# Preparing weight splits 2048 columns at a time, with the low part of 54 loads formed by an accumulating DMA

## The chip, the cores and the metric

The kernel runs on one core of one Trainium2 chip. The metric is the device time of one execution in microseconds (us), median over the runs. Lower is better.

## The reference, cut to what matters

Two transformer-like blocks act on 256 tokens of 1024 features in float32. The first has a chunked attention, a gated linear recurrence and a gated feed-forward layer, the second a gated token mixer, a stick-breaking attention and four gated feed-forward layers. Nearly all the arithmetic is products of activations with large weight matrices:

```python
u = jnp.einsum('bsd,de->bse', rmsnorm(h, g), w_in)      # 1024 x 7168
gate, up = jnp.split(h @ w_ffn_in, 2, axis=-1)          # 1024 x 5632, five times
x = x + scale * ((jax.nn.silu(gate) * up) @ w_ffn_out)  # 2816 x 1024, five times
```

The weights are used once each, so 250 MB of them stream through the core in one execution.

## The kernel before, in words

**Precision by splitting.** A weight w is split into a high part h, which is w rounded to the short float format fp32r, and a low part l = w - h. Activations are split in the same way. Each product is then three matmuls: h with the high activations, h with the low activations, and l with the high activations (`mm3`, L212 to L215). The third one of a triple is the first to need l.

**Groups.** `PLAN` (L67 to L93) lists 239 groups in the order of their use; a 240th load-sized transfer is there for the recurrence's gates. A group is one 1 MB load of 128x2048 weights (`raw`), made of two halves of 1024 columns. Most halves take 24 matmuls of 256 columns. Groups are numbered from 0; 40 to 72 are the first feed-forward layer, 73 to 105 the second, and so on. In a feed-forward layer two groups that write fresh `wk` banks (input weights) alternate with one group that adds to `acc` banks (output weights), so the pattern repeats every three groups.

**The weight pipeline.** SyncE (SP) issues the loads (`load`, L139), with three `raw` buffers. `prep` (L149 to L168) prepares one half: ScalarE copies `raw` to h (L162), and VectorE computes l = raw - h (L163). After the second half of a group its `raw` buffer is given up, and `load` issues the load three groups on. There are eight h buffers and eight l buffers of 1024 columns each. `refill` (L177) is called after each half that TensorE takes: it prepares up to two halves, as long as fewer than seven halves (four, for the first twelve halves) lie ahead of TensorE. So the second half of group g is asked for after the first half of group g-3, and the first half of group g half a group earlier.

**The order of the work.** The schedule is written by hand (`manual_schedule`): each engine runs its instructions in the order in which Python issues them. `group` (L199) issues a half's matmuls, then steps the generators that evict and process results (`rounds`, L184; two steps a half), then calls `refill`. So an engine's queue holds evictions and preparations in one fixed order, and an instruction that waits holds up all that stand behind it. In a feed-forward layer an eviction goes VectorE (L306, times the row factor), ScalarE (L738, silu), VectorE (L743), ScalarE (L309, high part), VectorE (L310, low part). GpSimd (POOL) does little: the power for the norms (`rpow`, L280), the loads of the attention bias (L467) and two fills behind each (L469), and three other small loads (L977, L982, L937).

**The start.** `block1` (L386 to L390) splits the inputs and prepares groups 0 and 1 in between, the first half in two pieces. Groups 2 and 3 are the first that `refill` prepares. The second feed-forward layer (L878) passes `more`, which keeps `refill` from preparing anything in some places (L750, L765), so that the statistics of two norms come first.

Of the kernel before, what the change touches and what calls it, by code (L numbers as in the profile page):

```python
# [9 lines left out]
F32 = mybir.dt.float32  # L10
F32R = mybir.dt.float32r
BF16 = mybir.dt.bfloat16
AF = mybir.ActivationFunctionType
# [7 lines left out]
NJ = FF // 128  # L21
NEG = -1e30

NB = 8
LA = NB - 1
NRAW = 3


# [38 lines left out]
def make_plan():  # L67
# [24 lines left out]

PLAN = make_plan()  # L93

PARAMS = [
    ("norm_mix_g", 8), ("conv_w", 32), ("conv_b", 8), ("b_r", 8), ("b_i", 8), ("lam", 8),
    ("b_merge", 16), ("norm_ffn_g", 8), ("final_norm_g", 8), ("ffn_norm", 32), ("mix_norm", 16),
# [9 lines left out]
class Builder:  # L107
# [14 lines left out]
        return self.ci // 2  # L122

    def take(self):
        h, l = self.hl.pop(self.ci)
        spec = PLAN[self.ci // 2][self.ci % 2]
        self.ci += 1
        return h, l, spec

    def sb(self, name, shape, dt=F32):  # L130
        return self.cp.tile(shape, dt, tag=name, name=name)
# [14 lines left out]
        if g == 4:  # L146
            self.nc.sync.dma_start(self.gw, self.dram["gates"])

    def prep(self, pieces=1):  # L149
        n = self.preps  # L150
        g, c = divmod(n, 2)
        if g >= len(PLAN):
            return
        self.preps += 1
        nc = self.nc
        raw = self.raw[g][:, c * 1024:(c + 1) * 1024]
        h = self.hlp.tile([128, 1024], F32R, tag="h", name="h")
        l = self.hlp.tile([128, 1024], F32R, tag="l", name="l")
        w = 1024 // pieces
        for i in range(pieces):  # L160
            s = slice(i * w, (i + 1) * w)
            nc.scalar.activation(h[:, s], raw[:, s], AF.Copy)  # L162
            nc.vector.tensor_tensor(l[:, s], raw[:, s], h[:, s].bitcast(F32), op=ALU.subtract)  # L163
        self.hl[n] = (h, l)
        if c == 1:
            del self.raw[g]
            if self.loads < g + 1 + NRAW:
                self.load()  # L168

    def spawn(self, gen):  # L170
        self.gens.append(gen)
# [2 lines left out]
        next(gen)  # L174
        self.gens.append(gen)

    def refill(self, most=2):  # L177
        """prepares the weights to come, more of them once the first loads have landed"""
        ahead = LA if self.ci > 12 else 4
        for _ in range(most):  # L180
            if self.preps < self.ci + ahead:
                self.prep()

    def rounds(self, n=2):  # L184
        for _ in range(n):
# [94 lines left out]
        self.nc.gpsimd.tensor_tensor(dst, src, self.mhalf[:, 0:src.shape[1]], op=ALU.pow)  # L280

    def bcast_mm(self, bank, half, col, start):
        """a factor per token (partition) to a row on every partition"""
        for t in range(2):
            self.mm(bank[:, half, t * 128:(t + 1) * 128], col[:, t:t + 1].to_broadcast([128, 128]), self.ident,
                    start and t == 0, True)

    def stats_a(self, pool=None, kv=False):
        """squares to the per-token factor column"""
        nc = self.nc  # L290
        self.st = (pool or self.acc)()
        self.R, self.rcol = (self.Rkv, self.rckv) if kv else (self.Rt, self.rc)
        self.stat_mm(self.sq[0], self.st, 0, True)
        nc.vector.tensor_scalar(self.v2, self.st[:, 0, 0:2], 1.0 / D, 1e-6, op0=ALU.mult, op1=ALU.add)
        self.rpow(self.rcol, self.v2)

    def stats_b(self):
        """the factors on every partition"""
        self.bcast_mm(self.st, 1, self.rcol, False)
        self.nc.scalar.activation(self.R, self.st[:, 1, :], AF.Copy)  # L300

# [58 lines left out]
        nc.gpsimd.memset(self.tiny, 2.0 ** -115)  # L360

    def warm_up(self):
        """keeps the tensor engine busy while the first operands are on their way"""
        nc = self.nc
        nc.vector.memset(self.SL["c"][:, 0:64], 0.0)
        junk = self.SL["c"][:, 0:64].bitcast(BF16)
        bank = self.wk()
        for _ in range(40):
            self.mm(bank[:, 0, 0:128], junk, junk, True, True)
        nc.scalar.preload_act_table_set("exp_and_others")  # L370
# [7 lines left out]
        for gi in range(2):  # L378
            self.group(kinds, lambda c, h, l, s: self.pe_k(h, l, s[2], self.XS, outs), fills=fills[gi])

    # ---------------------------------------------------------------- block 1
    def block1(self):
        nc, dram = self.nc, self.dram
        SA, SL, RR = self.SA, self.SL, self.RR
# [1 line left out]
        for p in range(4):  # L386
            self.split_h(p, self.X, g, self.XS)
            self.split_l(p, self.X, g, self.XS)
            self.prep(2 if p == 0 else 1)
        self.squares(self.X, self.sq)  # L390

        xr = SA.rearrange("p (a b) -> p a b", b=259)
# [6 lines left out]
        gb = SL["g"].rearrange("p (a b) -> p a b", b=256)  # L399
        ga = SL["h"].rearrange("p (a b) -> p a b", b=256)  # L400

        # xr
        w = ("A", "w_in")
        b = [self.wk(), self.wk()]
        self.start_k((("K", "w_in"),) * 2, [b[0][:, 0, :], b[0][:, 1, :], b[1][:, 0, :], b[1][:, 1, :]])
# [31 lines left out]
        for p in range(4):  # L437
            a_group(mul_ev(ga, p))

        # v, tokens on partitions  # L440
        V = SL["c"].rearrange("p (t c) -> p t c", c=1024)
        for cg in range(2):
            banks = [self.wk(), self.wk()]
# [9 lines left out]
                           lambda c, h, l, s: self.pe_nat(h, l, s[2], self.XS, banks),  # L453
                           end=(lambda: self.spawn(v_ev())) if gi else None)

        # attention state
        qk = self.carve("b", 0, 2, 512)
        PT = self.carve("b", 1024, 2, 384) + self.carve("d", 1536, 1, 384) + self.carve("f", 1536, 1, 384)
        bias = self.carve("d", 0, 2, 768)
# [82 lines left out]

        qk_group(0)

        # rnn_out
        accs = [self.acc() for _ in range(4)]
        for r in range(4):
            self.group((("R", "rnn_out"),) * 2,
# [10 lines left out]
        for j in range(1, 8):  # L559
            qk_group(j)  # L560

        # attn_out, merged with the recurrent branch
        accs2 = [self.acc() for _ in range(4)]
        MH, ML = RR[0], RR[1]
        for r in range(3):
# [13 lines left out]
        self.tail_group("attn_out", (6, 7), lambda k: (OH[:, k, :], OL[:, k, :]), accs2, merge, merge_l)  # L579
        self.drain()  # L580

        # w_o and the residual
        gf = lambda k: ("norm_ffn_g", k)
        for half in range(2):
            b = [self.wk(), self.wk()]
# [120 lines left out]
                    yield  # L706

    def tail_group(self, name, ks, zf, accs, fin, fin_l):
        """last two rows of weights, output by output, each pair finished as it comes"""
        g = self.gi  # L710
        assert [c[:3] for c in PLAN[g]] == [("R", name, k) for k in ks], (PLAN[g], name, ks)
        hl = [self.take()[:2] for c in range(2)]
        self.rounds(1)
        for p in range(4):
            for o in (2 * p, 2 * p + 1):
                for i, k in enumerate(ks):
                    s = slice(o * 128, o * 128 + 128)
                    zh, zl = zf(k)
                    self.mm3(accs[p][:, o % 2, :], hl[i][0][:, s], hl[i][1][:, s], zh, zl, start=False, stop=(i == 1))
            fin(p)  # L720
            if p:
                fin_l(p - 1)
        fin_l(3)
        self.rounds(1)
        self.refill()

    # ---------------------------------------------------------------- feed-forward
    def ffn(self, n, fin, fin_l, stats=None, nat=False, more=None):
        nc = self.nc
        a, r = ("A", f"{n}_in"), ("R", f"{n}_out")  # L730
# [56 lines left out]
        return accs  # L787

    def pe_rn(self, h, l, zh, zl, accs, first, last, banks=range(4)):
        """a row block of weights as the moving operand: tokens on partitions"""  # L790
        for b in banks:
            t, cg = divmod(b, 2)
            out = accs[b].rearrange("p a b -> p (a b)")
            s, ts = slice(cg * 512, cg * 512 + 512), slice(t * 128, t * 128 + 128)
            self.mm(out, zh[:, ts], h[:, s], first, False)
            self.mm(out, zh[:, ts], l[:, s], False, False)
            self.mm(out, zl[:, ts], h[:, s], False, last)
# [19 lines left out]
            self.split_l(p, self.X, g, xs)  # L817
        return fin, fin_l

    # ---------------------------------------------------------------- block 2  # L820
    def block2(self):
        nc, dram, P = self.nc, self.dram, self.par
        SA, SL, RR = self.SA, self.SL, self.RR

        # end of block 1: x2 = h * r1 * g1, next input x2 * r2 * g2
        XG = self.view("c", 4)

        def fin(p, bank):
# [71 lines left out]
        self.ffn("f3", fin, fin_l, stats=(lambda: self.stats_a(kv=True), sb3))  # L900
        self.squares(self.X, self.sq)

        # keys and values from the state before that feed-forward layer
        Kt = SL["c"][:, 0:512].rearrange("p (a b) -> p a b", b=256)
        Vt = SL["c"][:, 512:1024].rearrange("p (t c) -> p t c", c=256)
        kb, vb = self.acc(), self.acc()
# [33 lines left out]
        assert not self.gens  # L940

    def final_bank(self, b, bank):
        """the last norm and the output"""
        nc = self.nc
        t, cg = divmod(b, 2)
        flat = bank.rearrange("p a b -> p (a b)")
        part = lambda name, t, c: self.SL[name][:, (2 * t + c) * 512:(2 * t + c + 1) * 512]
        s0, s1, v, r = self.ss[:, t, 0:1], self.ss[:, t, 1:2], self.v2[:, t:t + 1], self.rc[:, t:t + 1]
        nc.scalar.activation(part("d", t, cg), flat, AF.Square, accum_out=s1 if cg else s0)  # L949
        nc.vector.tensor_tensor(part("f", t, cg), flat, self.gfin[:, cg * 512:(cg + 1) * 512], op=ALU.mult)  # L950
        if cg == 0:
            nc.vector.tensor_scalar(s0, s0, 1.0 / D, 1e-6, op0=ALU.mult, op1=ALU.add)
        else:
            nc.vector.tensor_scalar(v, s1, 1.0 / D, s0, op0=ALU.mult, op1=ALU.add)
            self.rpow(r, v)
        if b >= 2:
            t = b - 2
            r = self.rc[:, t:t + 1]
            nc.scalar.activation(part("f", t, 0), part("f", t, 0), AF.Copy, scale=r)  # L959
            nc.vector.tensor_scalar(part("f", t, 1), part("f", t, 1), r, None, op0=ALU.mult)  # L960
            for c in (1, 0):
                nc.sync.dma_start(self.dram["out"][t * 128:(t + 1) * 128, c * 512:(c + 1) * 512], part("f", t, c))

    def sgu(self, fin, fin_l):
# [29 lines left out]
                if c % 2:  # L994
                    yield

        # gate half, tokens on partitions
        def v_ev(banks, cg):
            sl = slice(cg * 512, (cg + 1) * 512)
            for t in range(2):  # L1000
# [42 lines left out]
        UH, UL = (RR[0], RR[1]), (RR[2], RR[3])  # L1043

        def mix(p):
            """token mixing of feature tiles 2p, 2p+1 and the product with u"""
            bank = self.wk()
            for f in range(2):
                c = 2 * p + f
# [203 lines left out]


def stick_order():
    """heads in the order of the tiles: two heads of neighbouring key/value heads each"""
    cols = []
    for T in range(8):
        kp, t = divmod(T, 4)
        for h in (2 * kp * 4 + t, (2 * kp + 1) * 4 + t):  # L1260
            cols.extend(range(h * 64, h * 64 + 64))
    return np.array(cols)
# [82 lines left out]
```

## Time and profile before

| what | us |
|---|---|
| median of the runs shown | 1462.57 |
| the runs (2) | 1462.52 and 1462.61 |
| profiled execution, span from first to last instruction | 1460.8 |
| TensorE busy in that span | 1451.3 |
| VectorE busy | 950.9 |
| ScalarE busy | 734.7 |
| GpSimd busy | 24.8 |

The profiled execution has no time of its own beside its span in what is shown; the median of the runs lies 1.8 us above the span, which is taken as what lies around it. Mean granted TensorE clock over the span: 0.999.

In the rows below, PE is TensorE's matmuls, PEld its weight loads, DVE VectorE, ACT ScalarE, POOL GpSimd and SP SyncE. "L163" is line 163 of the kernel. "l<-raw,h" means that l is written from raw and h. A timeline row begins with the start in us from the span's start and the length in us, and "x3" says that three like instructions in a row were merged into it.

### The profile page before, as it was taken

To read this page: it belongs to the slowest core of one execution; us is meant where nothing else is said; L and a number is where in the kernel's file an instruction comes from. 1 tells how busy PE (TensorE), PEld (TensorE's weight loads), DVE (VectorE), ACT (ScalarE), POOL (GpSimd) and SP (SyncE) were. 2 spreads that over 40 slices of the span, in tenths; PEclk is the share of its full clock that TensorE was granted. 3 is DMA by queue.
4 is the path that set the end of the run, shared out by engine and by line. 5 is a ranking of instruction groups with operands and counts; after the bars stand their busy time and mean duration, and the time that the engine had idled before them with its cause. 6 is when DMAs were issued, how large, how long until landed. Compare 5 with 4: busy or idle time off the path is not lost.

```text
span 1460.8 us, 26958 instructions
## 1 busy us (share of the span) xinstructions
PE 1451.3 (99%) x11548; PEld 1413.2 (97%) x11548; DVE 950.9 (65%) x1316; ACT 734.7 (50%) x1094; POOL 24.8 (2%) x57
## 2 busy tenths in 40 slices
PE   9999999999999999999999999999999999999998
PEld 9998999999999999998999999999999998999997
DVE  6976677665557765576775655567655576655563
ACT  5677465544445544455445444445444467544442
POOL 0000000000000000000000000000000000000000
PEclk9999999999999999999999999999999999999999
DMA  8555444454454555546444555544555542445451
GB/s 293 199 186 198 177 163 174 173 202 174 176 188 155 194 185 189 195 178 221 170 155 164 189 186 177 191 181 164 190 196 195 179 174 87 159 145 196 180 182 49
DMA packets 37624, 260.31 MB, mean 178 GB/s; under 512 B 4224, under 2 KB 4608, under 8 KB 7040
## 3 DMA queue, kind: packets, MB, share of 16 engines
q1 hardware_dynamic: 36288, 253.77, 48.7%
q0 software_dynamic: 1072, 4.72, 1.0%
q8 instruction: 90, 1.47, 0.4%
q14 instruction: 30, 0.25, 0.0%
q10 hardware_dynamic: 144, 0.10, 0.0%
HBM read 257.53 MB, written 1.05 MB: 177 GB/s over the span
## 4 chain that ended last, share of the span: by engine, by line
PE 99%; DMA 0%; ACT 0%; DVE 0%; SPq 0%; issue 0%; POOLq 0%; POOL 0%
PE wk L210 62%; PE acc L210 36%; DMA raw<-w 0%; PE acc L521 0%; PE wk L521 0%; ACT sf L959 0%; ACT sd L949 0%; DVE l L163 0%; ACT h L162 0%; SPq L352 0%; SPq L343 0%; DVE sf L950 0%; POOLq L1341 0%; POOL rc L280 0%; ACT sh L1134 0%
## 5 line engine op out<-in xcount | busy, mean ns | idle before, releaser
L163 DVE TENSOR_TENSOR l<-raw,h 128x1024 fp32r<-128x1024 f32 (+1 forms) x479 | 570.8, 1219 | 241.0 <-ACT h L162 240.4
L210 PE MATMUL wk<-xh,h 128*128 128x256 f32 x2272 | 646.8, 285 | 1.2 <-ACT h L162 1.2
L210 PE MATMUL wk<-xh,l 128*128 128x256 f32 x2272 | 643.9, 283 | 0.1
L210 PE MATMUL wk<-xl,h 128*128 128x256 f32 x2272 | 643.6, 283 | 0.0
L162 ACT ACTIVATE h<-raw 128x1024 fp32r<-128x1024 f32 (+1 forms) x479 | 485.7, 1044 | 64.6 <-PE acc L210 30.1
L210 PEld LDWEIGHTS wk<-xh,h 128*128 128x128 f32 x2272 | 436.7, 192 | 4.0 <-ACT h L162 1.8
L210 PEld LDWEIGHTS wk<-xl,h 128*128 128x128 f32 x2272 | 436.7, 192 | 0.5
L210 PEld LDWEIGHTS wk<-xh,l 128*128 128x128 f32 x2272 | 436.5, 192 | 0.6 <-DVE l L163 0.6
L210 PE MATMUL acc<-rr,h 128*128 128x256 f32 x2016 | 367.2, 284 | 0.0
L210 PEld LDWEIGHTS acc<-rr,h 128*128 128x128 f32 x2016 | 314.3, 192 | 1.9 <-issue 1.9
L210 PE MATMUL acc<-rr,l 128*128 128x256 f32 x1008 | 285.2, 283 | 0.0
L210 PEld LDWEIGHTS acc<-rr,l 128*128 128x128 f32 x1008 | 193.4, 192 | 0.0
L738 ACT ACTIVATE sa<-sa 128x256 f32<-128x256 f32 x110 | 45.4, 417 | 285.6 <-DVE sa L306 285.4
L309 ACT ACTIVATE rr<-sa 128x256 fp32r<-128x256 f32 (+1 forms) x122 | 52.7, 439 | 185.8 <-DVE sa L743 128.9
L306 DVE TENSOR_TENSOR sa<-wk,rt 128x512 f32<-128x512 f32 x92 | 62.3, 686 | 91.0 <-PE wk L210 73.1
L310 DVE TENSOR_TENSOR rr<-sa,rr 128x256 fp32r<-128x256 f32 (+1 forms) x122 | 54.2, 451 | 53.3 <-ACT rr L309 53.3
L210 PE MATMUL acc<-h,rr 128*128 128x512 f32 (+1 forms) x208 | 63.1, 374 | 0.0
L210 PEld LDWEIGHTS acc<-h,rr 128*128 128x128 f32 x208 | 38.7, 189 | 6.7
L258 ACT ACTIVATE xh<-x,par 128x256 fp32r<-128x256 f32 x56 | 25.2, 501 | 33.8 <-DVE x L316 18.6
L210 PE MATMUL acc<-l,rr 128*128 128x512 f32 (+1 forms) x104 | 38.9, 374 | 0.0
L743 DVE TENSOR_TENSOR sa<-sa 128x256 f32<-128x256 f32 x88 | 37.0, 428 | 0.0
L210 PE MATMUL wk<-rr,h 128*128 128x256 f32 x192 | 34.8, 283 | 0.0
(253 smaller groups left out, 970.2 us busy)
## 6 DMA issues: line engine op xcount, KB each, us to landing
raw<-w SPq DMA_DIRECT2D x237, 1024.0 KB, 4.9
sd<-bias POOLq DMA_DIRECT2D x8, 384.0 KB, 3.3
raw<-w SPq DMA_DIRECT2D x3, 512.0 KB, 8.3
sh<-gates SPq DMA_DIRECT2D x1, 1024.0 KB, 9.1
out<-sf SPq DMA_DIRECT2D x4, 256.0 KB, 2.1
x<-x SPq DMA_DIRECT2D x3, 256.0 KB, 7.4
raw<-w SPq DMA_DIRECT2D x2, 256.0 KB, 4.4
sa<-ws POOLq DMA_DIRECT2D x1, 512.0 KB, 3.7
```

The lines of the kernel that those rows point to most:

```text
L162: nc.scalar.activation(h[:, s], raw[:, s], AF.Copy)
L163: nc.vector.tensor_tensor(l[:, s], raw[:, s], h[:, s].bitcast(F32), op=ALU.subtract)
L210: self.nc.tensor.matmul(out, lhsT, rhs, start=start, stop=stop, skip_group_check=True)
L258: self.nc.scalar.activation(xs[0][:, k, :], src[p][:, f, :], AF.Copy, scale=self.par(*g(k)))
L306: self.nc.vector.tensor_tensor(dst, bank, self.Rpair(), op=ALU.mult)
L309: self.nc.scalar.activation(zh, src, AF.Copy)
L310: self.nc.vector.tensor_tensor(zl, src, zh.bitcast(F32), op=ALU.subtract)
L738: nc.scalar.activation(t[:, 0, :], t[:, 0, :], AF.Silu)
L743: nc.vector.tensor_tensor(t[:, 1, :], t[:, 0, :], t[:, 1, :], op=ALU.mult)
```

## The change

Each h and l buffer now holds a whole group: four buffers of 2048 columns in place of eight of 1024. `prep` prepares one group per call, `refill` calls it at most once per half, and the whole of group g is asked for after the first half of group g-3 (g-2 for the first twelve halves). The start keeps its pieces. For 54 groups, every fourth from 16 to 228, ScalarE first writes -h into the l buffer, then a DMA issued by GpSimd adds the raw weights to it (from the `raw` buffer for the 26 groups below 120, from HBM again for the 28 from 120 on), and ScalarE writes h. The other preparations are one ScalarE and one VectorE instruction of 2048 columns. Comments were removed.

```diff
-NB = 8
-LA = NB - 1
+NB = 4
 NRAW = 3
...
+DMA_L = {g: g < 120 for g in range(16, 232, 4)}
...
     def take(self):
-        h, l = self.hl.pop(self.ci)
-        spec = PLAN[self.ci // 2][self.ci % 2]
+        g, c = divmod(self.ci, 2)
+        h, l = (t[:, c * 1024:(c + 1) * 1024] for t in (self.hl.pop(g) if c else self.hl[g]))
         self.ci += 1
-        return h, l, spec
+        return h, l, PLAN[g][c]
...
-    def prep(self, pieces=1):
-        n = self.preps
-        g, c = divmod(n, 2)
-        if g >= len(PLAN):
+    def split(self, raw, h, l, s):
+        self.nc.scalar.activation(h[:, s], raw[:, s], AF.Copy)
+        self.nc.vector.tensor_tensor(l[:, s], raw[:, s], h[:, s].bitcast(F32), op=ALU.subtract)
+
+    def begin(self):
+        g = self.preps
+        self.preps += 1
+        self.hl[g] = tuple(self.hlp.tile([128, 2048], F32R, tag=n, name=n) for n in "hl")
+        return g
+
+    def release(self, g):
+        del self.raw[g]
+        if self.loads < g + 1 + NRAW:
+            self.load()
+
+    def prep(self):
+
+        if self.preps >= len(PLAN):
             return
...
+        g = self.begin()
+        raw, (h, l) = self.raw[g], self.hl[g]
+        if g in DMA_L:
+            self.nc.scalar.activation(l, raw, AF.Copy, scale=-1.0)
+            self.nc.gpsimd.dma_start(l, raw if DMA_L[g] else self.dram["w"][g], accum_op=ALU.add)
+            self.nc.scalar.activation(h, raw, AF.Copy)
+        else:
+            self.split(raw, h, l, slice(0, 2048))
+        self.release(g)
...
-    def refill(self, most=2):
-        """prepares the weights to come, more of them once the first loads have landed"""
-        ahead = LA if self.ci > 12 else 4
-        for _ in range(most):
-            if self.preps < self.ci + ahead:
-                self.prep()
+    def refill(self, most=1):
+
+        ahead = NB if self.ci > 12 else 3
+        if most and self.preps < (self.ci - 1) // 2 + ahead:
+            self.prep()
...
-            self.prep(2 if p == 0 else 1)
+            if p % 2 == 0:
+                g0 = self.begin()
+            for s in ((0, 512), (512, 1024)) if p == 0 else ((p % 2 * 1024, p % 2 * 1024 + 1024),):
+                self.split(self.raw[g0], *self.hl[g0], slice(*s))
+            if p % 2:
+                self.release(g0)
```

## Rows read from the trace of the kernel before

**Rows 1.** The page: busy time by engine, and shares of the chain that ended last.
```profile
PE 1451.3 (99%) x11548; PEld 1413.2 (97%) x11548; DVE 950.9 (65%) x1316; ACT 734.7 (50%) x1094; POOL 24.8 (2%) x57
...
PE 99%; DMA 0%; ACT 0%; DVE 0%; SPq 0%; issue 0%; POOLq 0%; POOL 0%
```

**Rows 2.** The chain in order of time: start us, length us, matmuls merged.
```profile
388.35 11.52 PE wk L210 x96
405.63 11.52 PE wk L210 x96
...
457.47 14.40 PE wk L210 x120
...
493.79 11.52 PE wk L210 x96
```

**Rows 3.** Groups of instructions by form: the two halves of a preparation.
```profile
L163 DVE TENSOR_TENSOR l<-raw,h 128x1024 fp32r<-128x1024 f32 x477 | 569.4, 1222 | 239.4 <-ACT h L162 238.9
L162 ACT ACTIVATE h<-raw 128x1024 fp32r<-128x1024 f32 x477 | 484.4, 1046 | 63.1 <-PE acc L210 30.1 <-PE wk L210 20.2 <-DMA raw<-w 5.6
```

**Rows 4.** Timeline of ScalarE at the start: h of groups 2 and 3.
```profile
18.25 2.01 ACT L162 ACTIVATE h<-raw 128x1024 fp32r<-128x1024 f32 x2 [0.81 <-DMA raw<-w]
20.74 2.01 ACT L162 ACTIVATE h<-raw 128x1024 fp32r<-128x1024 f32 x2 [0.49 <-DMA raw<-w]
```

**Rows 5.** Timeline of VectorE at the start: l of groups 2 and 3.
```profile
19.34 4.85 DVE L163 TENSOR_TENSOR l<-raw,h 128x1024 fp32r<-128x1024 f32 x4
```

**Rows 6.** Timeline of TensorE where group 2 begins: its first and third matmul.
```profile
20.41 0.28 PE L210 MATMUL wk<-xh,h 128*128 128x256 f32 x1
...
20.65 0.36 PE L210 MATMUL wk<-xh,l 128*128 128x256 f32 x1
```

**Rows 7.** DMA queues and issues: share of 16 engines, then KB each and median us to landing.
```profile
q1 hardware_dynamic: 36288, 253.77, 48.7%
...
raw<-w SPq DMA_DIRECT2D x237, 1024.0 KB, 4.9
```

**Rows 8.** Timeline of ScalarE in a feed-forward layer: preparations between evictions.
```profile
398.19 1.04 ACT L162 ACTIVATE h<-raw 128x1024 fp32r<-128x1024 f32 x1
...
401.45 1.04 ACT L162 ACTIVATE h<-raw 128x1024 fp32r<-128x1024 f32 x1
...
404.45 2.94 ACT L162 ACTIVATE h<-raw 128x1024 fp32r<-128x1024 f32 x3
```

**Rows 9.** Timeline of ScalarE: the second half's h of groups 20, 48 and 76.
```profile
122.03 1.05 ACT L162 ACTIVATE h<-raw 128x1024 fp32r<-128x1024 f32 x1
...
303.83 2.94 ACT L162 ACTIVATE h<-raw 128x1024 fp32r<-128x1024 f32 x3
...
466.71 2.94 ACT L162 ACTIVATE h<-raw 128x1024 fp32r<-128x1024 f32 x3
```

**Rows 10.** Timeline of ScalarE where groups 78 to 80 are prepared.
```profile
483.36 1.04 ACT L162 ACTIVATE h<-raw 128x1024 fp32r<-128x1024 f32 x1
486.03 0.42 ACT L309 ACTIVATE rr<-sa 128x256 fp32r<-128x256 f32 x1 [1.62 <-DVE sa L743]
486.35 1.99 ACT L162 ACTIVATE h<-raw 128x1024 fp32r<-128x1024 f32 x2
490.48 0.42 ACT L738 ACTIVATE sa<-sa 128x256 f32<-128x256 f32 x1 [2.14 <-DVE sa L306]
```

**Rows 11.** Timeline of VectorE in the same stretch.
```profile
485.58 0.42 DVE L743 TENSOR_TENSOR sa<-sa 128x256 f32<-128x256 f32 x1
...
489.70 0.68 DVE L306 TENSOR_TENSOR sa<-wk,rt 128x512 f32<-128x512 f32 x1
```

**Rows 12.** Timeline of GpSimd: one load of the attention bias, and the fills behind it.
```profile
190.06 0.54 POOL L467 DMA_DIRECT2D sd<-bias  x1 [3.90 <-DVE att L488]
193.51 0.34 POOL L469 MEMSET sd<- 64x128 f32 x2 [2.91 <-DMA sd<-bias]
```

**Rows 13.** Who waited for whom, SyncE's queue: us in total, times, longest us.
```profile
SPq L145 <- DVE l L163: 1239.1, 227, 12.8
```

More of the change, by code (lines that the diff above doesn't have):

```diff
@@ L147, in load @@
             self.nc.sync.dma_start(self.gw, self.dram["gates"])
-    def prep(self, pieces=1):
-        n = self.preps
-        g, c = divmod(n, 2)
-        if g >= len(PLAN):
-            return
[L154 to L168, printed above, removed]
+    def split(self, raw, h, l, s):
[12 more added lines that the diff above has]
+        if self.preps >= len(PLAN):
+            return
+        g = self.begin()
[7 more added lines that the diff above has]
+        self.release(g)
     def spawn(self, gen):
```

## Prediction

> **What bounds the kernel now.** I read the page first. TensorE is busy for 1451.3 of 1460.8 us, and the chain that ended last is 99% TensorE [rows 1]. A busy TensorE need not be one at its peak, so I looked next at the chain in order of time: its pieces hold 96 matmuls in 11.52 us, again and again, which is 0.120 us a matmul [rows 2]. A group of 48 takes 5.76 us, and the next one follows at once. The weights are prepared far enough ahead almost everywhere: VectorE needs 1.22 us and ScalarE 1.05 us for a half, so 2.44 and 2.09 us for a group [rows 3], well under 5.76. The reader is to see that preparation is off the path. Less work for VectorE can give back at most what TensorE idles now, 1460.8 - 1451.3 = 9.5 us, and most of that is the start and the end, which the change leaves alone. The question is only where a preparation becomes late.
>
> **Part 1: whole groups in one instruction.** Of a 1024-column instruction, two merged ones show the length of the second: ScalarE's pair takes 2.01 us, so one of 2048 columns takes about 1.9 us, and VectorE's four take 4.85 us, so one of 2048 takes about 2.3 us [rows 4, 5]. Nothing is dearer, but l is ready only when all of it is. In most places this hides behind a lead of two or three groups. Two places have none.
>
> Group 2: ScalarE starts its h when the load lands, at 18.25 [rows 4]. VectorE starts l at 19.34, so its first half ends at about 20.56 [rows 5]; TensorE's third matmul of the group, the first to need l, starts at 20.65 after a touch of waiting [rows 6]. Afterwards h ends at 18.25 + 1.9 = 20.15, in time for the first matmul at 20.41, and l at 20.2 + 2.3 = 22.5. TensorE waits 22.5 - 20.65 = 1.85 us. Group 3 follows from the load that lets h start at 20.74 [rows 4]; l ends near 24.9, before group 3 begins at 26.7 or later. So +1.85 us once.
>
> Group 78: TensorE starts it near 487.9 (half-way between the pieces that start at 457.47 and 493.79, and checked by 5.76 us a group backwards from the second [rows 2]). Its h starts at 483.36 [rows 10]; then h ends at 485.3 and l at 487.6, half a microsecond before the third matmul. I cost it at nothing; if VectorE is late by more, it is paid in full.
>
> **Part 2: the accumulating DMA.** It takes 54 x 2.3 = 124 us from VectorE, worth nothing on the path, and gives ScalarE 54 x 1.9 = 103 us, so that such a group costs it 3.8 us of 5.76. The new chain is: TensorE frees the buffer, ScalarE writes -h (1.9 us), GpSimd issues (0.1 us until it starts), the DMA lands D us later, TensorE's third matmul goes. ScalarE's instruction stands where the second half's h stood, because both are asked for after the first half of group g-3.
>
> The room for D, steady state: in a feed-forward layer the second half's h starts at 398.19 (group 65), 404.45 (group 66, first of three) and soon after the start of a group in the third case [rows 8]. Group 65 begins near 411.2: the pieces of the chain start with the first group of each pair, at 388.35 for 61 and 405.63 for 64 [rows 2], within 0.2 us. So D may be 411.2 + 0.24 - 398.19 - 2.0 = 11.3 us, for the next class 10.8, and over 14 for the third. Where the ScalarE queue runs late it is less, by the same sum: group 20, whose h starts at 122.03 and which begins at 130.7, 6.9; group 48 (303.83, 313.3), 7.7; group 76 (466.71, 475.4), 6.9 [rows 9]. Tightest is group 80. Its -h stands behind a row of things: h of 78 to 485.3, VectorE's l of 78 to 487.6, then the multiply that was at 485.58 to 488.0 [rows 11], ScalarE's high part of it to 488.5 and h of 79 to 490.4 [rows 10], l of 79 to 492.7, the eviction that was at 489.70 to 493.4 [rows 11], silu to 493.8 [rows 10], then -h to 495.7. TensorE needs l at 499.6. D may be 3.8 us.
>
> D itself: no row shows an accumulating DMA. From below it is a plain load of the same 1 MB, 4.9 us to landing. A megabyte costs 0.487 x 1460.8 / 253.77 x 1.05 = 2.94 us of all 16 engines [rows 7]. An accumulation reads two megabytes and writes one. If only the second read adds, D = 4.9 + 2.94 = 7.8. If a concurrent raw load adds its share as well, 10.8; if the write stops being pipelined too, 13.7, the upper end. I take 7.8, nearest to the row of the plain load, which already pipelines its read with its write. Stalls at 7.8: group 80 4.0, group 76 0.9, group 20 0.9, group 48 0.1, together 5.9 us. At 4.9 only group 80 pays, 1.1. At 10.8 I sum the same differences over all 54 starts and find 17 groups and 27 us; at 13.7, 33 groups and 109 us.
>
> The Trainium skill ("Collectives: The Full Stack", section "The bandwidth ceiling: the fold count and why AG ≠ RS ≠ AR") says that an add inside the DMA engines is slow not for the arithmetic but because it reads two sources through one read queue, and so runs at half a copy's rate. With its page "DMA: Bandwidth & Descriptors", section "Anatomy of one DMA — SWDGE (gpsimd) path" (a fixed 2.0 us and bytes over 436 GB/s), an estimate from these pages is D = 2.0 + 2 x 2.4 = 6.8 us, and the sum would be 2.9 us less than mine. No run here shows it yet.
>
> **New waits and who stands behind them.** GpSimd's DMA waits for -h. Behind it stand the norm's power and the loads of the attention bias. The power comes half a group after such a DMA has been issued, and an attention bias lands with its fill 3.8 us after its issue (190.06 to 193.85 [rows 12]) while its reader comes about a group later, so a delay of 1 to 3 us is covered. SyncE's load of g+3, which waited for VectorE's l until now, 12.8 us at the longest [rows 13], waits for the DMA's landing in the 26 groups with a raw source: by the steady state 4.7 + 2.0 + 7.8 = 14.5 us after group g-3 begins, then 4.9 us of load, 19.4 in all, against a preparation asked for at 17.3 + 0.9 or later. ScalarE may wait a microsecond there, with more than two groups of lead left. From group 120 on the raw buffer is free after ScalarE alone, for 28 MB more from HBM. The DMA engines' share rises from 49% by 54 x 2 to 3 x 2.94 us, that is to 70 or 80%.
>
> **The sum.** 1460.8 + 1.85 + 5.9 = 1468.6 for the span; with the 1.8 us by which the runs' median lies above it, 1470.4 us, 0.5% slower and within what a measurement of this kernel can tell from no change, which I set at 2% or 29 us.
>
> **The rivals.**
> 1. The accumulating DMA is slow and becomes the bound (D of 10.8 us and more). For it: three streams instead of one, beside loads that keep the engines half busy, and a dozen groups with only 11.3 us of room. Against it: 8 KB rows, and most groups have 11 to 15 us. It decides from D = 10.9 on, where the sum passes 1492; at 13.7 it is 1462.6 + 1.85 + 108.5 = 1573. Past 15 us nearly every one of the 54 pays the excess.
> 2. Everything is hidden: D near 4.9, and ScalarE reaches group 80 earlier because it has half as many preparations to start. Then only group 2 pays: 1464.5. For it: the plain load's 4.9. Against it: the second read.
> 3. VectorE's relief lets TensorE go faster. All of TensorE's idle time is 9.5 us, so the least it could give is 1453; to pass 2% the 0.120 us a matmul would have to fall, and nothing in the change touches a matmul.
> 4. The DMA doesn't relieve anything because GpSimd holds it back: in the attention its queue waits for landings (2.91 us before a fill [rows 12]). Behind such a wait D grows by about 3.4 us for four groups (20 to 32), whose room is 6.9 to 18: at most 4 us more, 1474.
>
> **How the numbers follow.** Forecast (D between 5.5 and 10.8, rival 4 in it) 0.54; rival 2 0.24; rival 1 0.21; rival 3 0.01. The likeliest gives 1470.4, with a range of its own from 1466 to 1492. The lower end of the range is just under rival 2's no cost, 1461. Above, I leave out the far part of rival 1, some 0.15, and stop at 1515, where D is about 11.7. Faster by over 2%: 0.01. Within 2%: 0.78. Slower: 0.21.
>
> **What would show each step right or wrong.** TensorE's third matmul of group 2 starts near 22.5. The issues section shows a GpSimd line l<-raw with 26 issues and l<-w with 28; its landing time is D, and 7.8 is my number. The waits list TensorE's weight loads behind that DMA at group 80 first, then 76 and 20, and nowhere in the steady layers. VectorE's share falls to about 55% and ScalarE's rises to about 55% (merging halves saves some 0.15 us each time), the 0.120 us stays. I am wrong if the DMA's landing is over 11 us, or if ScalarE or VectorE queue so that an eviction, not l, is late.

## The result, and the profile after

The changed kernel takes 1487.26 us (1486.87 and 1487.65), against 1462.57: a ratio of 1.0169, 95% interval 1.0139 to 1.0198. That is 24.7 us slower, still inside 2%, inside the range given, and 16.9 us above the forecast of 1470.4. The span of the profiled execution is 1485.8 us, 25.0 more than before.

The page of the changed kernel, busy time by engine and the chain that ended last, which answer to [rows 1]:

```profile
PE 1460.3 (98%) x11548; PEld 1418.5 (95%) x11548; DVE 814.6 (55%) x1025; ACT 808.2 (54%) x911; POOL 73.7 (5%) x111
...
PE 85%; DMA 4%; ACT 4%; DVE 4%; issue 1%; SPq 0%; POOL 0%; POOLq 0%; ACTq 0%
```

VectorE lost 136 us of work and TensorE's count of matmuls is the same, yet the chain that was 99% TensorE now has 15% of other things in it. DMA, ScalarE and VectorE stand there with 4% each: the path runs back through preparations, because TensorE stopped for them. A share of the chain isn't a loss, since most of that preparation lies beside matmuls; it says where to look. The list of waits says how much. Waits of TensorE's weight loads in the changed kernel (us in total, times, longest us):

```profile
PEld wk L218 <- DMA l<-raw: 4.1, 3, 3.1
...
PEld wk L218 <- DMA l<-w: 3.6, 2, 2.0
PEld wk L218 <- DVE sb L537: 2.5, 2, 2.2
PEld wk L218 <- DVE l L152: 2.3, 3, 1.0
...
PEld acc L218 <- DMA l<-raw: 1.6, 1, 1.6
PEld acc L218 <- DVE rr L318: 1.5, 2, 1.2
...
PEld acc L218 <- ACT sd L536: 1.0, 1, 1.0
```

Beside VectorE's own l (2.3 us), two kinds of line are to be seen. Six waits, 9.3 us, end with a landing of the accumulating DMA. Another three lines (`sb`, `rr`, `sd`, 5.0 us) name operands that the change doesn't touch: intermediates of the attention and of other stages that VectorE or ScalarE now delivers too late.

I then paired the two traces half group by half group and took the difference of TensorE's starts. It is flat almost everywhere (a group takes 5.76 us in both) and rises in steps:

| where | step, us | what TensorE waited for |
|---|---|---|
| start and group 2 | -0.15 + 0.87 | VectorE's l of group 2 |
| groups 31, 32, 33 | 0.33 + 1.41 + 2.71 | attention, `sd` and `sb` |
| group 34 | 1.49 | nothing; half clock |
| group 45; group 168 | 0.41; 1.21 | `rr` |
| groups 20, 76 | 0.59, 0.51 | DMA l<-raw |
| group 80 and 81 | 5.30 + 0.46 | DMA l<-raw, then half clock |
| group 108 | 2.09 | DMA l<-raw, then the norm's power |
| group 132 | 1.60 | DMA l<-w |
| group 172 | 3.56 | DMA l<-w, then half clock |
| groups 23, 202 to 204 | 0.42, 0.43 | not followed up |
| after TensorE's last work | 1.8 | end of the program |

They add up to the 25.0 us.

**The tightest place, group 80.** Timeline of the changed kernel, from VectorE's l of group 79 to TensorE's restart (start us, length us; in brackets idle time and what ended it):

```profile
498.81 2.29 DVE L152 TENSOR_TENSOR l<-raw,h 128x2048 fp32r<-128x2048 f32 x1 [1.38 <-ACT h L151]
...
502.12 1.90 ACT L172 ACTIVATE l<-raw 128x2048 fp32r<-128x2048 f32 x1
...
504.32 0.90 POOL L173 DMA_DIRECT2D l<-raw  x1 [19.25 <-ACT l L172]
...
508.00 0.28 PE L218 MATMUL wk<-xh,h 128*128 128x256 f32 x1
508.12 0.28 PE L218 MATMUL wk<-xl,h 128*128 128x256 f32 x1
511.32 0.58 PE L218 MATMUL wk<-xh,l 128*128 128x256 f32 x1 [2.91 <-DMA l<-raw]
511.69 0.42 PE L218 MATMUL wk<-xh,h 128*128 128x256 f32 x1
511.91 0.41 PE L218 MATMUL wk<-xl,h 128*128 128x256 f32 x1
```

The first two matmuls of the group go, the third needs l and stands. GpSimd's issue begins 2.2 us after -h begins (1.9 for -h, 0.3 to react), and the DMA lands 6.95 us later. After the wait the matmuls begin 0.22 us apart where they were 0.12 apart before it. The windows of the same stretch show why (us; length, then busy time and count of PE, PEld, DVE, ACT and POOL; then granted clock, DMA share, GB/s):

```profile
499.80:505.56 5.76, 5.76 (x50) 5.76 (x49) 2.33 (x3) 3.76 (x3) 0.90 (x1) 1.00 0.63 216
505.56:511.32 5.76, 2.85 (x25) 2.64 (x23) 3.78 (x3) 4.17 (x4) 0.00 (x0) 0.92 0.90 182
511.32:517.20 5.88, 5.88 (x27) 5.88 (x28) 2.59 (x4) 0.83 (x2) 0.00 (x0) 0.50 0.85 304
```

In the third window TensorE is busy throughout and issues 27 matmuls where the first has 50. The granted clock is 0.50, 1.2 GHz in place of 2.4. A wait can thus have a second price that no list of waits shows.

**The DMA itself.** Queues and issues of the changed kernel, which answer to [rows 7] (share of 16 engines; KB each, median us to landing):

```profile
q1 hardware_dynamic: 36288, 253.77, 47.2%
q0 software_dynamic: 8848, 61.35, 20.8%
...
raw<-w SPq DMA_DIRECT2D x237, 1024.0 KB, 5.3
l<-w POOLq DMA_DIRECT2D x28, 1024.0 KB, 9.4
l<-raw POOLq DMA_DIRECT2D x26, 1024.0 KB, 7.7
sd<-bias POOLq DMA_DIRECT2D x8, 384.0 KB, 6.5
```

Landing takes 7.7 us from SBUF and 9.4 from HBM at the median, and GpSimd's other loads land later too: the bias 6.5 us in place of 3.3. The chain in order of time has two of the late landings as pieces of its own, those of groups 132 and 172:

```profile
815.02 9.29 DMA l<-w
...
1046.16 13.56 DMA l<-w
```

**The merged instructions.** Groups of instructions in the changed kernel (busy us, mean ns | idle before), which answer to [rows 3]:

```profile
L152 DVE TENSOR_TENSOR l<-raw,h 128x2048 fp32r<-128x2048 f32 (+2 forms) x188 | 423.7, 2258 | 272.5 <-ACT h L151 272.0
...
L151 ACT ACTIVATE h<-raw 128x2048 fp32r<-128x2048 f32 (+2 forms) x188 | 352.0, 1876 | 90.4 <-DMA raw<-w 43.2
...
L172 ACT ACTIVATE l<-raw 128x2048 fp32r<-128x2048 f32 x54 | 102.8, 1904 | 23.8 <-PE acc L218 19.9
L174 ACT ACTIVATE h<-raw 128x2048 fp32r<-128x2048 f32 x54 | 102.4, 1896 | 0.0
```

VectorE's idle time before l, 272.5 us over 188 instructions, is 1.45 us each, where it was 0.50 for each half (239.4 over 477, [rows 3]). A whole h must end before any l can begin.

### The profile page after: what moved, and what is told of

The parts are those of the page before. It is cut to its first block, busy times and chain, and to the rows that moved or that the text cites. A ratio compares the mean times of both kernels' runs of the same rounds, so it can differ in the third digit from the quotient of the medians.

```text
span 1485.8 us, 26329 instructions
## 1 busy us (share of the span) xinstructions
PE 1460.3 (98%) x11548; PEld 1418.5 (95%) x11548; DVE 814.6 (55%) x1025; ACT 808.2 (54%) x911; POOL 73.7 (5%) x111
## 3 DMA queue, kind: packets, MB, share of 16 engines
q1 hardware_dynamic: 36288, 253.77, 47.2%
q0 software_dynamic: 8848, 61.35, 20.8%
q8 instruction: 90, 1.47, 0.4%
HBM read 286.89 MB, written 1.05 MB: 194 GB/s over the span
## 4 chain that ended last, share of the span: by engine, by line
PE 85%; DMA 4%; ACT 4%; DVE 4%; issue 1%; SPq 0%; POOL 0%; POOLq 0%; ACTq 0%
PE wk L218 53%; PE acc L218 32%; DVE l L152 2%; ACT h L151 2%; DMA l<-w 2%; DMA l<-raw 1%; ACT l L172 1%; DMA sa<-ws 1%; DMA raw<-w 1%; DVE sa L314 0%; DVE sa L703 0%; DVE sa L756 0%; ACT sb L278 0%; DVE rr L318 0%; DVE sf L498 0%
## 5 line engine op out<-in xcount | busy, mean ns | idle before, releaser
L152 DVE TENSOR_TENSOR l<-raw,h 128x2048 fp32r<-128x2048 f32 (+2 forms) x188 | 423.7, 2258 | 272.5 <-ACT h L151 272.0
L151 ACT ACTIVATE h<-raw 128x2048 fp32r<-128x2048 f32 (+2 forms) x188 | 352.0, 1876 | 90.4 <-DMA raw<-w 43.2
L172 ACT ACTIVATE l<-raw 128x2048 fp32r<-128x2048 f32 x54 | 102.8, 1904 | 23.8 <-PE acc L218 19.9
L174 ACT ACTIVATE h<-raw 128x2048 fp32r<-128x2048 f32 x54 | 102.4, 1896 | 0.0
L173 POOL DMA_DIRECT2D l<-w x28 | 24.4, 873 | 601.4 <-ACT l L172 570.3
L173 POOL DMA_DIRECT2D l<-raw x26 | 22.8, 878 | 575.1 <-ACT l L172 575.1
```

The source lines that it names most:

```text
L151: self.nc.scalar.activation(h[:, s], raw[:, s], AF.Copy)
L152: self.nc.vector.tensor_tensor(l[:, s], raw[:, s], h[:, s].bitcast(F32), op=ALU.subtract)
L172: self.nc.scalar.activation(l, raw, AF.Copy, scale=-1.0)
L173: self.nc.gpsimd.dma_start(l, raw if DMA_L[g] else self.dram["w"][g], accum_op=ALU.add)
L174: self.nc.scalar.activation(h, raw, AF.Copy)
```

## The experiments

The measured medians stand against the runs of the kernel before on the same chip, 1462.47 to 1462.68 us.

**1. Only the merging: no accumulating DMA.**

```diff
-DMA_L = {g: g < 120 for g in range(16, 232, 4)}
+DMA_L = {}
```

> No accumulating DMA; VectorE forms every low part, whole groups at a time. Theory A (the landing of the DMA and ScalarE's extra instruction cause the loss): only group 2's wait of 0.8 us is left, span about 1462, time 1463.5 to 1465. Rival B (2048-column instructions standing in front of evictions cause the losses in the attention's end, 5.9 us, at groups 45 and 168, 1.6 us, beside group 2): about 1471. The last 1.9 us at the end of the program, between SyncE's last drain and GpSimd's answer, go by A if they belong to the DMAs.

Measured: 1471.45 us, ratio 1.0064 (1.0049 to 1.0079). So 8.8 of the 24.7 us have nothing to do with the DMA. The steps are at group 2 (0.79), 31 to 34 (0.48, 1.41, 3.40, 0.78), 45, 135 and 168 (0.41, 0.42, 1.21). In the attention the cause can be read off VectorE. First the kernel before, VectorE's timeline in the attention:

```profile
201.69 2.36 DVE L163 TENSOR_TENSOR l<-raw,h 128x1024 fp32r<-128x1024 f32 x2 [1.26 <-ACT h L162]
209.94 2.36 DVE L163 TENSOR_TENSOR l<-raw,h 128x1024 fp32r<-128x1024 f32 x2 [1.26 <-ACT h L162]
```

Then the merge-only kernel:

```profile
205.16 2.29 DVE L152 TENSOR_TENSOR l<-raw,h 128x2048 fp32r<-128x2048 f32 x1 [2.06 <-ACT h L151]
213.92 2.29 DVE L152 TENSOR_TENSOR l<-raw,h 128x2048 fp32r<-128x2048 f32 x1 [2.06 <-ACT h L151]
```

Before, an l came every 8.25 us, TensorE's pace there. Now it comes every 8.76. In two pieces VectorE forms the first low part while ScalarE makes the second high part; in one piece they follow each other, and waiting plus work grow from 1.26 + 2.36 to 2.06 + 2.29, by 0.73 us a group. Some 0.2 of that was spare, the other 0.51 lengthens a loop that goes through both engines, until TensorE waits for `sd`, which ScalarE copies behind such an h, and for `sb`, which VectorE copies behind such an l. The steps at groups 33 and 34 hold some half clock too: from 231.6 to 235.1 us the granted clock is 0.51, and the same two groups lose 4.18 us here and 2.72 in experiment 3, where the clock stays at 1.00.

**2. The DMAs stay, the other groups in two pieces.**

```diff
-            self.split(raw, h, l, slice(0, 2048))
+            for c in range(2):
+                self.split(raw, h, l, slice(c * 1024, (c + 1) * 1024))
```

> The 54 DMAs stay; the other groups are prepared by two instructions of 1024 columns an engine, in the same places of the queues. Theory A: only group 2's 0.8 us and a little go, 1485 to 1486. Rival B: the attention's end (5.9 us), groups 45 and 168 (1.6 us) and group 2 (0.8 us) go, about 1479.

Measured: 1474.02 us, 1.0076 (1.0061 to 1.0091), lower than either theory. The steps in the attention are gone, and with them the half clock there. But the step of 80 shrank too, from 5.76 to 1.61, and that of 172 from 3.56 to 0.82, and neither is followed by half clock. At 80 the DMA's room had itself been eaten by merged instructions ahead of -h in ScalarE's queue: -h starts 9.8 us after group 77 begins, against 11.4. The two losses are not a sum; the long instructions also took room from some of the landings.

**3. No accumulating DMA for group 80 alone.**

```diff
-DMA_L = {g: g < 120 for g in range(16, 232, 4)}
+DMA_L = {g: g < 120 for g in range(16, 232, 4) if g != 80}
```

> 53 DMAs, group 80 goes to VectorE. If only the wait of 3.1 us at group 80 goes and the half clock after it is something else: 1484. If the half clock of 6.8 us follows from that wait, its 2.5 us go too: 1481.5, and the clock record shows no low stretch near 510 us.

Measured: 1480.83 us, 1.0124 (1.0109 to 1.0139). The step at 80 is gone with its half clock. Others moved: 76 now costs 1.33, 136 1.23, 172 only 1.79. And this profile has no half clock behind the 1.8 us wait of group 33. That the time is near the 1481.5 expected is therefore partly chance: the gain at groups 34 and 172 was not expected, nor the losses at 76 and 136. The windows behind that wait, first the changed kernel:

```profile
227.50:233.50 6.00, 4.00 (x30) 3.02 (x29) 4.31 (x9) 4.29 (x10) 0.00 (x0) 1.00 0.47 171
233.50:239.00 5.50, 5.50 (x35) 5.50 (x36) 0.71 (x2) 4.47 (x5) 0.90 (x1) 0.69 0.80 246
```

Then without group 80's DMA, which at this point has done nothing different yet:

```profile
227.50:233.50 6.00, 3.99 (x30) 3.01 (x29) 4.09 (x8) 4.29 (x11) 0.00 (x0) 1.00 0.48 169
233.50:239.00 5.50, 5.50 (x49) 5.50 (x48) 0.98 (x2) 4.12 (x4) 0.90 (x1) 1.00 0.78 243
```

The wait is the same (4.00 and 3.99 us busy of 6), the clock behind it is not: 35 matmuls against 49 in 5.5 us. So a wait of about 2 us may bring half clock or not.

**4. Each DMA 1.9 us later: h before -h.**

```diff
+            self.nc.scalar.activation(h, raw, AF.Copy)
             self.nc.scalar.activation(l, raw, AF.Copy, scale=-1.0)
             self.nc.gpsimd.dma_start(l, raw if DMA_L[g] else self.dram["w"][g], accum_op=ALU.add)
-            self.nc.scalar.activation(h, raw, AF.Copy)
```

> ScalarE writes h before -h, so each of the 54 DMAs starts 1.9 us later. Theory A with the slack of each landing as measured (l landed after its need at groups 20, 76, 80, 108, 132, 172, and less than 1.9 us before it at 48, 52, 136, 208 and a few more): 11 us at the first six, 5 us at the others and 4 to 8 us more of half clock where a wait now reaches 2 us: 1505 to 1512. Rival B (the landing is not what matters): within 3 us of 1487.

Measured: 1522.65 us, 1.0402 (1.0384 to 1.0421). The direction and the groups are right: the groups that were late in the changed kernel lose more (132 7.70, 80 6.97, 172 5.99, 108 4.30), and 48 and 136, in time by 0.88 and 0.45 us, now lose 1.87 and 5.99. The size was underestimated. The landings from HBM became longer too, 11.3 us at the median where they took 9.4, so that six groups that had 2.2 to 4.0 us to spare (144, 156, 180, 188, 192, 220) are late as well. Five waits were followed by half clock: the attention's 1.8 us and those of 80, 132, 136 and 172, in which TensorE stood for 3.6 to 5.3 us. Those of 20, 76, 108 and 144, 2.0 to 2.2 us, were not. So 1.9 us each cost more than 1.9 us. That a late group moves the next DMA against the loads beside it may have a part; no run isolates it. Waits of TensorE's weight loads in this kernel:

```profile
PEld wk L218 <- DMA l<-w: 13.6, 5, 5.2
PEld wk L218 <- DMA l<-raw: 10.1, 3, 5.5
PEld acc L218 <- DMA l<-w: 7.3, 5, 2.3
PEld acc L218 <- DMA l<-raw: 4.8, 3, 2.4
```

**5. All 54 from SBUF.**

```diff
-DMA_L = {g: g < 120 for g in range(16, 232, 4)}
+DMA_L = {g: True for g in range(16, 232, 4)}
```

> All 54 accumulating DMAs read the raw tile in SBUF; none reads the weights a second time from HBM. Theory H (a landing from HBM is the longer one, 9.4 us against 7.7, and that is why groups 132 and 172 are late): the steps of 132 (1.60) and 172 (3.56, 1.5 of it half clock) go, the rest stays: 1487.3 - 5.2 = about 1482. Theory C (what makes those landings long is the raw load that runs beside them, whatever the source): 132 and 172 stay late by 1 to 2 us, and the raw tile is now held until the landing, so later loads start later: 1485 to 1490.

Measured: 1481.66 us (1480.56 to 1483.49), 1.0131 (1.0116 to 1.0147). The steps of 132 and 172 are gone: their landings take 6.95 and 11.56 us in place of 9.29 and 13.57. So with SBUF as the source both land in time. The source is not isolated by this, though. A raw buffer that the DMA reads is held until the landing, so that the next raw load no longer runs beside it. The trace of the changed kernel shows how much this may matter: 0.8 MB or more of raw loads start during each of the 28 landings from HBM, and under 0.6 MB during 19 of the 26 from SBUF. Those 19 took 7.3 us at the median, but six from SBUF with 0.8 to 1.1 MB beside them 10.8; the 17 from HBM with 0.8 to 1.0 MB took 9.2, the other 11, with more, 11.4. With as much beside it, a landing from HBM was not the longer one. (A longer landing also meets more of the loads, so this is a sign and no proof.) In this experiment group 172, with 1.05 MB beside it from SBUF, still needs 11.56. One thing came by itself: in this profile group 80 waits as before (2.90 us), without half clock behind it. Its step is 3.15 us, so of the 5.76 in the changed kernel 2.6 were the clock.

**6. Merged tiles, but two pieces, and no DMA.** The edits of 1 and 2 together.

> No accumulating DMA; the tiles stay 2048 wide and are asked for a group at a time, but ScalarE and VectorE form them in two pieces of 1024 each. Theory L (the 8.8 us of the merge-only kernel are the length of the instructions): nearly all of it goes, 1462.7 to 1464. Theory O (they come from asking for a whole group at one place and from the buffers being freed a group at a time): the attention's 5.9 us stay, 1469 to 1471.

Measured: 1462.91 us, 1.0003 (0.9994 to 1.0013): no difference. Tiles of a whole group, asked for at one place and freed together, cost nothing. The cost in experiment 1 is the length of the instructions, with the half clock behind one of its waits.

**7. Merged instructions, except in the attention.**

```diff
-            self.split(raw, h, l, slice(0, 2048))
+            n = 2 if 28 <= g <= 37 else 1
+            for c in range(n):
+                self.split(raw, h, l, slice(c * 2048 // n, (c + 1) * 2048 // n))
```

with `DMA_L = {}` as in 1.

> No accumulating DMA, one instruction for 2048 columns, except in groups 28 to 37, where two pieces of 1024 are formed. Theory L: the steps of groups 31 to 34 (.48, 1.41, 3.40, .78 in the merge-only kernel) go, while group 2 (.8), 45 (.4), 135 (.4) and 168 (1.2) stay: 1471.5 - 6 = about 1465.5. If the loss comes from ScalarE and VectorE being late by what happened before group 28, at least 3 of the 6 us stay: 1468 or more.

Measured: 1465.48 us, 1.0021 (1.0011 to 1.0030), as expected. VectorE's timeline has the pace of before back (8.25 us):

```profile
194.64 2.36 DVE L152 TENSOR_TENSOR l<-raw,h 128x1024 fp32r<-128x1024 f32 x2 [1.26 <-ACT h L151]
202.89 2.36 DVE L152 TENSOR_TENSOR l<-raw,h 128x1024 fp32r<-128x1024 f32 x2 [1.26 <-ACT h L151]
```

Ten groups in two pieces give back 6.0 of the 8.8 us. What stays is group 2 (1.06), 45, 135 and 168, at the places of experiment 1.

**8. Two pieces, and only three accumulating DMAs.**

```diff
-DMA_L = {g: g < 120 for g in range(16, 232, 4)}
+DMA_L = {52: True, 56: True, 60: True}
```

with the edit of 2.

> Two pieces of 1024 everywhere, and only three accumulating DMAs, for groups 52, 56 and 60, all of them over 1000 us before the end; 56 and 60 have room, 52 was in time by 0.6 us. Theory E (the 1.9 us more between TensorE's last work and the end of the program come with any accumulating DMA in it): last instruction of ScalarE to the end 5.4 us, the time 1464.5. Theory N (they come with the number of such DMAs, or with those near the end): 3.5 us there and 1462.7.

Measured: 1464.10 us, 1.0009 (0.9999 to 1.0018). Inconclusive between the two theories: from the end of ScalarE's last instruction to the end of the span there are 4.5 us, 1.0 more than without such DMAs (3.5), 0.9 less than with 54 (5.4). The three landed in 7.0 us, with 6 to 8 us to spare.

**9. 43 accumulating DMAs where there is room, two pieces elsewhere.**

```diff
-DMA_L = {g: g < 120 for g in range(16, 232, 4)}
+DMA_L = {g: g < 120 for g in (
+    16, *range(52, 73, 3), *range(91, 104, 3), *range(112, 128, 3), *range(142, 161, 3),
+    *range(178, 197, 3), 201, 203, 208, *range(218, 237, 3))}
```

with the edit of 2.

> 43 accumulating DMAs, each for a group of a steady layer whose -h is asked for at least 14 us before TensorE needs l (none at 20, 76, 80, 108, 132 or 172), and two pieces of 1024 in all other groups. If the loss of the changed kernel is made of late landings, long instructions, half clock behind the waits, and a tail at the end, only the tail is left: the kernel with two pieces and no such DMA took 1462.9, and 1.0 (three DMAs) to 1.9 us (54) more between the last ScalarE work and the end make it 1464 to 1465; TensorE waits nowhere for an l. If the DMAs also cost by their traffic, in raw loads that land later or in evictions held up, 1467 or more.

Measured: 1464.03 us, 1.0012 (1.0002 to 1.0022), as expected. The page of this kernel:

```profile
PE 1451.5 (99%) x11548; PEld 1413.4 (97%) x11548; DVE 855.8 (59%) x1230; ACT 809.1 (55%) x1094; POOL 62.6 (4%) x100
...
PE 98%; DVE 1%; DMA 0%; ACT 0%; issue 0%; SPq 0%; POOLq 0%; POOL 0%
...
raw<-w SPq DMA_DIRECT2D x237, 1024.0 KB, 5.0
l<-w POOLq DMA_DIRECT2D x27, 1024.0 KB, 9.4
l<-raw POOLq DMA_DIRECT2D x16, 1024.0 KB, 7.4
```

The landings are as long as in the changed kernel (9.4, 7.4), their longest 13.1 us, but none is waited for; the narrowest is in time by 1.0 us. The chain is TensorE again and the traffic costs next to nothing. What is left, 1.6 us, is the tail of 1.0 us and two steps, 0.2 us at group 33 and 0.4 at 168, that experiment 6 has without any such DMA. VectorE does 95 us less than before and the time is not shorter: its relief is worth nothing here. No version beat the kernel before.

## Why the prediction was right and where it was wrong

**TensorE is the bound, nothing to win: right.** The spacing stayed 0.120 us and rival 3 had nothing to take. Experiment 9, with VectorE at 59% and no time won, shows it.

**Group 2, 1.85 us: right in kind, less than half the size.** The timeline of the changed kernel where group 2 is prepared:

```profile
17.07 1.90 ACT L151 ACTIVATE h<-raw 128x2048 fp32r<-128x2048 f32 x1
19.00 2.29 DVE L152 TENSOR_TENSOR l<-raw,h 128x2048 fp32r<-128x2048 f32 x1
...
21.34 0.39 PE L218 MATMUL wk<-xh,l 128*128 128x256 f32 x1 [0.68 <-DVE l L152]
```

The durations came out as predicted (1.9 and 2.3), but the load landed at 16.49 and not at 18.23, h began at 17.07 and not at 18.25 [rows 4], and TensorE waited 0.68 us. I had taken the landing of an early load from one execution as fixed.

**"In most places this hides behind a lead of two or three groups. Two places have none": wrong, 6.8 us.** This is the first step that failed. I had asked at which groups TensorE waits for l. The long instructions did their harm elsewhere: in the attention, where ScalarE and VectorE work alternately with little to spare, they lengthened their common loop by 0.51 us a group (experiment 1), and TensorE waited for an eviction. My last sentence named that sign ("if ScalarE or VectorE queue so that an eviction, not l, is late") and priced it at nothing: by that sign the account was wrong, although the time lies in the range. Experiments 6 and 7 show that it is the length alone and where it is paid.

**Group 78 at nothing: right.** No step there.

**The room, and D of 7.8 us.** Room is here the time from the start of GpSimd's issue to the moment when TensorE wants l.

| group | room predicted | room after | landing after | loss predicted | landing less room |
|---|---|---|---|---|---|
| 80 | 3.8 | 3.9 | 6.95 | 4.0 | 3.0 |
| 76 | 6.9 | 6.8 | 7.26 | 0.9 | 0.45 |
| 20 | 6.9 | 7.4 | 7.86 | 0.9 | 0.44 |
| 48 | 7.7 | 7.8 | 6.94 | 0.1 | none |
| 108 | not named | 7.6 | 9.03 | 0 | 1.46 |
| 132 | not named | 7.8 | 9.29 | 0 | 1.47 |
| 172 | not named | 11.6 | 13.57 | 0 | 1.93 |

The queue sums were good: the four rooms I gave came out within 0.5 us, the tightest within 0.1, although GpSimd began its issue 0.3 us after -h and not 0.1. The order 80, 76, 20 is right, and the 26 landings from SBUF have the median I took (7.7 against 7.8). **What failed is that D was one number.** It is 6.9 to 7.9 us in the four places I named, 9.0 and 9.3 at 108 and 132, and 13.6 at 172, where four raw loads were under way and 2.5 MB of them started before the landing. At 108 no raw load ran beside it, but the 512 KB load `sa<-ws`, issued half a microsecond behind, did. Landings from SBUF can be long too (11.7 and 12.4 us at 44 and 52, in time because the room there was wide). I gave "if a concurrent raw load adds its share as well, 10.8" as an upper case for all 54; it should have been weighed for each place, by the loads beside it. How much of a late landing is the loads beside it and how much the HBM source was seen (experiment 5), not isolated. The named groups lost less than the 5.9 predicted, about 4.3 without the clock, the three unnamed ones 5.6 more.

The Trainium skill ("Collectives: The Full Stack", section "The bandwidth ceiling: the fold count and why AG ≠ RS ≠ AR") explains that a reduce-scatter between cores runs at half the rate of an all-gather by the second read that its add in the DMA engines needs. The trace agrees in size, and no run shows the cause: q0's 61.35 MB cost 20.8% of the changed kernel's span, and with three such DMAs its 7.87 MB cost 2.0% of 1462.6 us, so 53.5 MB cost (309.0 - 29.3) / 53.5 = 5.2 us of all engines a megabyte, against 0.472 x 1485.8 / 253.77 = 2.8 for the plain loads, 1.9 times. The estimate of 6.8 us made from the pages is met only by the quickest landings, 6.9.

**"A delay of 1 to 3 us is covered" behind GpSimd's queue: mostly right.** The bias loads take 3.2 us longer at the median, and TensorE never waits for them. At group 108 it failed by little. GpSimd's timeline in the changed kernel:

```profile
667.45 0.86 POOL L173 DMA_DIRECT2D l<-raw  x1 [27.52 <-ACT l L172]
667.99 0.89 POOL L990 DMA_DIRECT2D sa<-ws  x1
677.79 1.10 POOL L991 TENSOR_SCALAR_AFFINE_SELECT sa<-sa 128x1024 f32<-128x1024 f32 x1 [8.91 <-DMA sa<-ws]
678.86 0.71 POOL L288 TENSOR_TENSOR rc<-v,mhalf 128x2 f32<-128x2 f32 x1
```

The load `sa<-ws`, issued right behind the accumulating DMA, lands after 9.7 us where it took 3.7, the select waits for it, and the norm's power stands behind both. TensorE waits 0.3 us for that power.

**Not foreseen at all: half clock, 5.7 us, and the tail, 1.8 us.** The clock behind the waits of groups 33, 80 and 172 costs 1.5, 2.6 and 1.6 us (the step less the wait). Of the tail, taken from ScalarE's last instruction to the end of the span, I know only that it comes with the accumulating DMAs: 3.5 us without any (before and experiments 1, 6, 7), 4.5 with 3 and with 43, 5.3 to 5.7 with 53 or 54. Neither their number nor their place alone explains these, and the cause stays open.

**The sum.** In place of 1.85 + 5.9 = 7.75 us stand: long instructions 6.8 (group 2 in it), landings 9.9, half clock 5.7, tail 1.8 and 0.85 not followed up, together 25.0. As one number for all, rivals 1 and 2 (D over 10.9, D near 4.9) are refuted by the landings: 13 of the 54 took more than 10.9 us, none was waited for but 172's, and none took less than 6.9. Rival 4 is refuted by GpSimd's issues, which began 0.3 us after the end of -h at groups 20 to 32.

That the time lies inside the range is luck. The range reaches so high because of a D near 10.8 or more at all 54 places; the median landing was 7.7 us from SBUF and 9.4 from HBM. Of the 25.0 us, the two kinds of loss that the sum had, group 2 and the late landings, make 10.6; the other 14.4 it had at nothing.

## What to carry to other kernels

An instruction made twice as long is not free when its sum stays the same: where two engines hand pieces to each other, look for the loop whose period is nearly the bound's, and count there the work that now runs in series. For a transfer with a deadline, work out the room place by place, as here, and give each place its own landing time, by what runs beside it; experiment 9 shows that such DMAs cost nearly nothing where the room is there. And when the bound engine is TensorE, price a wait of 2 us at up to twice its length.

## What the runs showed of the hardware that was not expected

Behind a wait TensorE may run on at 1.2 GHz: 27 matmuls in 5.88 us where it issues 50 at 2.4. Whether it does is not set by the wait alone. The same wait of 2.9 us at group 80 was followed by half clock in the changed kernel and not with all sources in SBUF; the same 1.8 us at group 33 was followed by it in the changed kernel and not without group 80's DMA. In the changed kernel the waits shorter than 1.5 us were not, and in experiment 4 four waits of 2.0 to 2.2 us were not either. The Trainium skill ("TensorE: Matmul & The Clock Gate", section "Part 1: The HAM clock gate (the "warmup" mystery)") says that the monitor behind the clock runs freely and doesn't start with the kernel, so that the moment of a change varies; these pairs agree with that and don't show it.

GpSimd's loads landed late right behind an accumulating DMA: 512 KB issued half a microsecond behind one took 9.7 us in place of 3.7, and the four bias loads issued as closely behind one 8.2 to 8.8 us, the four others 3.4 to 4.9, where all eight took 3.1 to 3.7 before.

The program's end came 0.9 to 2.2 us later in every kernel that had accumulating DMAs, in experiment 8 with the last of them over 1000 us back.
